# A third column tile in the first product of a sparse-attention and retention block, and a different split of its last steps

## The chip, the cores and the metric

The kernel runs on one core of one Trainium2 chip. The metric is the time of one execution on the device in microseconds (us); lower is better. A time given for a kernel is the median of several runs. Beside it stands the profile of one execution, whose span runs from the first to the last instruction.

## The reference

One layer of a streaming encoder for 512 tokens of width 2048, all in float32. Cut to what matters here:

```python
h = rmsnorm(x, norm_gain)                       # 512 x 2048
aq, ak, av, az, iq, ik, iw, rq, rk, rv, rz, ga, gb = split(h @ w_in)
# iq: 16 heads x 64, ik: 64 (layer-normed), iw: 16
index = sum_over_heads(relu(iq . ik) * iw)      # which 128 keys each query may see
a = sparse_attention(aq, ak, av, top_k(index), rel_bias) * silu(az)
b = retention(rope(rq), rope(rk), rv) * silu(rz)
r = x + (sigmoid(ga) * (a @ w_a_out) + sigmoid(gb) * (b @ w_b_out)) @ w_o
y = r + (p @ w_ple) * sigmoid(r @ w_ple_gate)
out = rmsnorm(y, final_gain)                    # 512 x 2048
```

The change concerns the very first product (the columns for `ik`, `iw` and the first `iq` heads) and the very last step (the final norm of the last tokens and the stores of the output).

## The kernel before

**Number format and layout.** Channels lie on the 128 partitions and the 512 tokens along the free dimension, so x is 16 tiles `xk` of 128 x 512 (256 KB each). Every float32 operand of a product is split into a high part in a reduced format and the rest: `x_split(k)` has ScalarE write `hh` (x times the norm weight `ng`, line 385) and VectorE write `hl` (line 386). Weights are loaded by SyncE's queue into raw tiles (line 115), then split by ScalarE into `wh` (line 136) and by VectorE into `wl` (line 141). One product step is three matmuls: high x high (line 196), high weight x low input (197), low weight x high input (198). The gain of each token, 1/rms, is applied later, so the product can start before the norm is known. `rms_acc` squares each `xk` on ScalarE (line 367) and adds the squares on GpSimd (even k) and VectorE (odd k, line 372).

**Weights come in blocks.** `block(src, chunks, cols)` cuts a weight matrix into units of so many of the 16 k-steps. `split_to(n)` emits the split of all units below n, `load_to(n)` their loads. `wh` and `wl` have three buffers each.

**The step queue.** The order of the work is written by hand. `gemms` (lines 177 to 202) runs over the 16 k-steps, and within each over its column tiles ("jobs"):

```python
for s in order:
    for ps, seq, (_, w, parts, c, _) in zip(pss, seqs, jobs):
        i, k = seq[s]
        if k == 0:
            split_to(i + (ahead or AHEAD) - (late and s > 0))
            load_to(i + AHEAD + LOADS)
        ...                     # three matmuls
        step()
```

After each job of each step, `step()` takes one item from the list `todo` (an item may be `None`) and emits it, so `todo` weaves the other engines' work into the matmul order. `later(n, f)` emits f n steps on. Each engine executes its own instructions in the order in which they are emitted. A list `bg` of background work (the later inputs, the top-k rounds, the bias masks) is drawn from when `todo` has nothing, every few steps.

**The first product.** Loads of `xk` and of the unit weights `w_ik` alternate on SyncE's queue, after the 20 KB of norm weights `g_sb` (line 338). The product has two column tiles: 80 columns (`ps_ikw`: the key of the indexer and its head weights, 512 tokens) and 128 columns (`ps_iq`: two indexer heads, tokens 128 to 511). `w_ik` has 208 columns in units of 2, 2, 4, 4 and 4 k-steps. While the loads arrive, ten warm-up matmuls run on zeros (line 380). Then seven more products give the other 14 indexer heads, tile by tile (`u_iq[1]` to `u_iq[7]`, two units of 8 k-steps each); `iq_split` copies each result out of PSUM with two ScalarE and two VectorE instructions (lines 436 to 439). Behind that, `todo` holds the norm (`f_sum`, `f_rnat`), the keys (`f_keys1` to `3`) and the index scores (`index_tile`).

**The last step.** The first 12 of 16 output channel tiles (`MF`) are ready for all tokens; for tokens 384 to 511 (`C3`) the last 512 channels are computed the other way round, with tokens on partitions (`ps_tg`, `ps_tw`). Their tail is a chain: for two halves of 256 columns a multiply and an add on VectorE (lines 1252, 1253) and a square with a row sum on ScalarE (line 1254); then 1/rms on GpSimd (`rl`, line 1259); its broadcast over PSUM by TensorE (`bb`, line 1263); a store of those 512 channels (`yb`, line 1265); and a multiply of the 12 other tiles by the broadcast, one of four on GpSimd and three on VectorE (lines 1273, 1275), stored by SyncE four tiles at a time (`yo`, line 1276). Earlier, `a_out` has scaled and stored tokens 0 to 383 (lines 1232 to 1238).

Of the kernel before, what the change touches and what calls it, by code (L numbers as in the profile page):

```python
# [13 lines left out]
AF = mybir.ActivationFunctionType  # L14
OP = mybir.AluOpType

L = 512
D = 2048
KT = D // 128
# [15 lines left out]
def block_kernel(tc, xT, pT, posb, posq, w_in, w_v, w_ik, w_a, w_b, w_o, w_ple, w_gate,  # L35
                 w_gt, w_pt, fgb, tab, gains, cst, dec, out, out_a, out_b):
    nc = tc.nc
    pe, dve, act, pool, sp = nc.tensor, nc.vector, nc.scalar, nc.gpsimd, nc.sync

    with contextlib.ExitStack() as ctx:  # L40
# [22 lines left out]
        def tok(t):  # L63
            return slice(128 * t, 128 * t + 128)
# [14 lines left out]
        def block(src, chunks, cols=128):  # L79
            ids, k0 = [], 0  # L80
            for nk in chunks:
                ids.append(len(units))
                units.append((raw(src, k0, nk, cols), None, nk, cols))
                k0 += nk
            return ids
# [67 lines left out]
        todo = collections.deque()  # L153
# [27 lines left out]
        def gemms(jobs, ahead=None, order=None, each=None):  # L181

            pss = [P(j[4]) for j in jobs]
            seqs = [ksteps(j[0]) for j in jobs]
            late = order is not None
            order = order or range(len(seqs[0]))
# [6 lines that stand above are left out]
                    h, l = loaded[i]  # L193
                    a, b = parts[s][0][:, c], parts[s][1][:, c]
                    o = ps[:w.stop - w.start, c]
                    pe.matmul(o, h[:, k, w], a, start=(s == order[0]), stop=False)  # L196
                    pe.matmul(o, h[:, k, w], b, start=False, stop=False)  # L197
                    pe.matmul(o, l[:, k, w], a, start=False, stop=(s == order[-1]))  # L198
                    step()
                if each is not None:  # L200
                    each(s)
            return pss
# [108 lines left out]
        K8 = (8, 8)  # L311
        col = lambda g, m: w_in[g + m]
        AQ, AK, AZ, IQ, RQ, RK, RZ, GA, GB = 0, 8, 16, 24, 32, 40, 48, 56, 72
        u_ik = block(w_ik, (2, 2, 4, 4, 4), 208)
        u_iq = [None] + [block(col(IQ, m), K8) for m in range(1, 8)]
        u_rv, u_av = ([block(w_v[i], (2,) * 8, 512) for i in g] for g in ((0, 1), (2, 3)))
        u_r, u_g = [], []
        for h in range(NH):
# [16 lines left out]


        g_sb = cp.tile([128, 40], F32, name="g_sb")
        sp.dma_start(g_sb, gains)
        ng, fg, gn = g_sb[:, 0:16], g_sb[:, 16:32], g_sb[:, 32:40]
        xs = []  # L340
        for k in range(KT):
            if k in (1, 2, 4, 8, 12):
                load_to(state["raw"] + 1)
            if k < 10:
                t = U("xk")
                sp.dma_start(t, xT[:, k, :])
                xs.append(t)
            elif k % 2 == 0:
                t = B("xk2")
                sp.dma_start(t[:, 0:1024].rearrange("p (a c) -> p a c", a=2), xT[:, k:k + 2, :])  # L350
                xs += [t[:, 0:512], t[:, 512:1024]]
# [68 lines left out]

        for k in range(2, KT):
            todo.append(lambda k=k: x_split(k))
            if k in (4, 5):
                todo.append(None)
            if k == 11:
                todo.extend([None] * 5)
        for k in range(KT):
            todo.extend([lambda k=k: rms_acc(xs[k], k), None])

        ps_ikw, ps_iq0 = gemms([(u_ik, slice(0, 80), hparts, ALL, "ps_ikw"),  # L430
                                (u_ik, slice(80, 208), hparts, slice(128, L), "ps_iq")], 2)

        def iq_split(ps):
            ta = U("ta", F32R)
# [7 lines left out]
        R = {}  # L442
        kraw = U("kraw")
        act.activation(kraw[:80, :], ps_ikw[:80, :], AF.Copy)
        ix = iq_split(ps_iq0)

        def f_sum():
            dve.tensor_add(acc[0], acc[0], acc[1])
# [123 lines left out]
                dve.scalar_tensor_tensor(a, rl[:, :ln], wq[:, t, n:n + 1], a, op0=OP.mult, op1=OP.add)  # L572

        def index_tile(m, ix):
            todo.extend(N3)
            for s in range(2):
                for t in range(1, NT):
                    todo.append(lambda s=s, t=t: index_score(2 * m + s, ix[s], t))

        index_tile(0, ix)  # L580
        for m in range(1, 8):
            ix = iq_split(gemm(u_iq[m], hparts, "ps_iq", slice(128, L)))
            index_tile(m, ix)

# [663 lines left out]
        drain()  # L1248
        sq = U("sq")
        for i in range(2):  # L1250
            c = slice(256 * i, 256 * i + 256)
            dve.tensor_mul(s[:, c], pw[:, c], s[:, c])
            dve.tensor_add(s[:, c], s[:, c], rn[:, c])
            act.activation(sq[:, c], s[:, c], AF.Square, accum_out=r3[:, i:i + 1])
# [9 lines left out]
        act.activation(s, s, AF.Copy, scale=rl)  # L1264
        sp.dma_start(out_b, s)
        b3 = U("b3")
        act.activation(b3[:, 0:128], bb[0][:, 0:128], AF.Copy)
        for q in range(MF // 4):
            o = U("yo")
            for i in range(4):  # L1270
                m = 4 * q + i
                if i == 3:
                    pool.tensor_mul(o[:, tok(i)], ys[m][:, C3], b3[:, 0:128])
                else:
                    dve.tensor_mul(o[:, tok(i)], ys[m][:, C3], bb[1][:, 0:128])
            sp.dma_start(out[:, 4 * q:4 * q + 4, C3], o.rearrange("p (a c) -> p a c", a=4))


MF = 12
# [19 lines left out]
def _layout(x, p, positions, w_in, norm_gain, w_a_out, w_b_out, w_o, ret_gn_gain,  # L1299
            w_ple, w_ple_gate, rel_bias, final_gain):  # L1300
    import numpy as np
    f32 = np.float32

    def tiles(w, c=128):
        k, n = w.shape
        return np.ascontiguousarray(w.reshape(k // 128, 128, n // c, c).transpose(2, 1, 0, 3))

    def chans(v):
        return v.reshape(-1, 128).T

    w = np.asarray(w_in)[0]
    o = {}
    o["xT"] = np.ascontiguousarray(np.asarray(x)[0].T.reshape(KT, 128, L).transpose(1, 0, 2))
    o["pT"] = np.ascontiguousarray(np.asarray(p)[0, 0].T.reshape(2, 128, L).transpose(1, 0, 2))
    pos = np.asarray(positions)[0]
    o["posb"] = np.ascontiguousarray(np.broadcast_to(pos[None, :], (128, L)))
    o["posq"] = np.ascontiguousarray(np.repeat(pos.reshape(128, 4).T, 32, axis=0))
    o["w_in"] = np.concatenate([tiles(w[:, a:b]) for a, b in
                                ((0, 2048), (3072, 5120), (5200, 7248), (8272, 13392))])
    o["w_v"] = np.concatenate([tiles(w[:, a:a + 1024], 512) for a in (7248, 2048)])  # L1320
    o["w_ik"] = np.ascontiguousarray(
        np.concatenate([w[:, 5120:5200], w[:, 4096:4224]], axis=1).reshape(KT, 128, 208).transpose(1, 0, 2))
    o["w_a"] = tiles(np.asarray(w_a_out)[0])
    o["w_b"] = tiles(np.asarray(w_b_out)[0])
    o["w_o"] = tiles(np.asarray(w_o)[0])
    o["w_ple"] = np.ascontiguousarray(
        np.asarray(w_ple)[0].reshape(2, 128, 16, 128).transpose(1, 2, 0, 3).reshape(128, 32, 128))
    o["w_gate"] = tiles(np.asarray(w_ple_gate)[0])
    o["w_gt"] = tiles(np.asarray(w_ple_gate)[0][:, 1536:], 512)
    o["w_pt"] = tiles(np.asarray(w_ple)[0][:, 1536:], 512)  # L1330
    o["fgb"] = np.ascontiguousarray(np.broadcast_to(np.asarray(final_gain)[None, 1536:], (128, 512)))
    tab = np.asarray(rel_bias)
    t = np.zeros((128, 65), f32)
    for q in range(4):
        for b in range(31):
            t[32 * q + b, 8 * q:8 * q + 8] = tab[ROW[b]]
            if b:
                t[32 * q + b, 32 + 8 * q:40 + 8 * q] = tab[ROW[b - 1]]
        t[32 * q:32 * q + 32, 64] = [-1e9] + THR[1:] + [1e9]
    o["tab"] = t  # L1340
    o["gains"] = np.ascontiguousarray(np.concatenate(
        [chans(np.asarray(norm_gain)[0]), chans(np.asarray(final_gain)), chans(np.asarray(ret_gn_gain)[0])], axis=1))
    c = np.zeros((128, 130), f32)
    c[:, :128] = np.eye(128)
    c[:, 128] = np.tile((10000.0 ** (-np.arange(64) / 64.0)).astype(f32), 2)
    c[:, 129] = math.pi / 2
    o["cst"] = c
    s = np.arange(128)[:, None]
    q = np.arange(128)[None, :]
    dec = np.zeros((128, NH, 257))  # L1350
    for h in range(NH):
        g = math.log(1.0 - 2.0 ** (-5.0 - h))
        dec[:, h, :128] = np.where(q // 64 >= s // 64, np.exp(g * np.abs(q - s)), 0.0) * 128.0 ** -0.5
        dec[:, h, 128:256] = np.exp(g * (q + 1.0))
        dec[:, h, 256] = np.exp(g * (127.0 - s[:, 0])) * 128.0 ** -0.5
    o["dec"] = dec.astype(f32)
    return o
# [30 lines left out]
```

## Time and profile before

| | |
|---|---|
| time, median of 3 runs | 1690.11 us (1689.55 to 1690.82) |
| the profiled execution's own time | 1689.83 us |
| its span | 1688.1 us |
| TensorE (PE) busy | 1675.0 us, 99% |
| VectorE (DVE) busy | 1275.3 us, 76% |
| ScalarE (ACT) busy | 863.4 us, 51% |
| GpSimd (POOL) busy | 213.4 us, 13% |
| granted TensorE clock | 0.998 of full |
| moved by DMA | 355.86 MB, 211 GB/s on average |

PEld is TensorE's weight load, which overlaps its matmuls; SPq is the queue of SyncE, which issues most transfers. A timeline row gives the start in us from the span's start, the duration, the engine, the line and operation, the tile written and read, and in brackets how long the engine had been idle and what ended that. Matmuls are pipelined: a 128 x 512 matmul is shown with 0.39 us, but the next one starts 0.23 us after it. So for TensorE the distance between starts counts, not the shown duration.

### The profile page before, as it was taken

What the parts mean: (1) busy time and instruction counts of PE and PEld (TensorE: products, weight loads), DVE (VectorE), ACT (ScalarE), POOL (GpSimd) and SP (SyncE); (2) the same over time, 40 slices, a digit from 0 to 9 for tenths busy, and PEclk for the clock granted to TensorE, in tenths of its full rate; (3) what the DMA queues carried; (4) which work ended last, traced back from release to release, by engine and by line L of the source; (5) the groups of instructions that cost most, each with busy time, mean ns of one, the idle gap of its engine ahead of it and who ended that gap; (6) DMA issues with size and microseconds to landing.
All of it is one profiled execution on the core that took longest, in us unless ns stands there. A gap on an engine that the chain in (4) does not pass through costs nothing.

```text
span 1688.1 us, 25020 instructions
## 1 busy us (share of the span) xinstructions
PE 1675.0 (99%) x9334; PEld 1453.5 (86%) x9334; DVE 1275.3 (76%) x2014; ACT 863.4 (51%) x1278; POOL 213.4 (13%) x216
## 2 busy tenths in 40 slices
PE   9999999999999999999999999999999999999997
PEld 7988888888888888888888888888888888888896
DVE  7787988887887887887887777687768877864453
ACT  7464523555555555555555555566644444463342
POOL 3100000111111111111331111100000111112222
PEclk9999999999999999999999999999999999999999
DMA  7438989788787788787988879998566788733222
GB/s 288 125 105 297 361 323 329 184 223 223 167 224 199 196 215 234 169 211 210 271 219 234 220 197 243 242 360 288 180 204 187 189 229 218 201 118 100 87 63 100
DMA packets 135369, 355.86 MB, mean 211 GB/s; under 512 B 14800, under 2 KB 27088, under 8 KB 135248
## 3 DMA queue, kind: packets, MB, share of 16 engines
q1 hardware_dynamic: 102640, 256.22, 44.0%
q0 software_dynamic: 21376, 77.60, 25.4%
q10 hardware_dynamic: 11232, 20.45, 3.3%
q8 instruction: 73, 1.20, 0.3%
q14 instruction: 48, 0.39, 0.1%
HBM read 301.26 MB, written 52.95 MB: 210 GB/s over the span
## 4 chain that ended last, share of the span: by engine, by line
PE 94%; DVE 3%; ACT 1%; DMA 1%; issue 0%; SPq 0%; POOL 0%; DVEq 0%; ACTq 0%
PE ps_p L258 23%; PE ps_v L258 15%; PE ps_r L258 8%; PE ps_q L258 8%; PE ps_vn L702 3%; PE ps_vn L701 3%; PE ps_vn L703 3%; PE ps_w L196 3%; PE ps_w L197 3%; PE ps_w L198 3%; PE ps_pg L198 3%; PE ps_pg L196 3%; PE ps_pg L197 3%; PE ps_iq L196 1%; PE ps_iq L197 1%; PE ps_iq L198 1%
## 5 line engine op out<-in xcount | busy, mean ns | idle before, releaser
L141 DVE TENSOR_TENSOR wl<-wraw,wh 128x1024 fp32r<-128x1024 f32 (+2 forms) x459 | 560.5, 1229 | 203.5 <-ACT wh L136 197.3
L136 ACT ACTIVATE wh<-wraw 128x1024 fp32r<-128x1024 f32 (+2 forms) x459 | 474.2, 1042 | 272.5 <-DVE wraw L143 132.9
L104 POOL DMA_DIRECT2D wraw<-w_in x120 | 106.3, 961 | 844.2 <-DVE wl L141 437.1
L224 ACT ACTIVATE e<-ps_p 128x512 f32<-128x512 f32 x144 | 86.1, 598 | 164.6 <-PE ps_p L258 162.4
L258 PE MATMUL ps_p<-hs,wh 128*128 128x512 f32 x640 | 161.4, 394 | 0.0
L258 PEld LDWEIGHTS ps_p<-hs,wh 128*128 128x128 f32 x640 | 114.9, 189 | 21.3 <-issue 0.7
L701 PE MATMUL ps_vn<-wh,hh 128*128 128x512 f32 x256 | 99.7, 390 | 0.0
L703 PE MATMUL ps_vn<-wh,hl 128*128 128x512 f32 x256 | 99.7, 389 | 0.0
L702 PE MATMUL ps_vn<-wl,hh 128*128 128x512 f32 x256 | 99.7, 389 | 0.0
L258 PE MATMUL ps_p<-hs,wl 128*128 128x256 f32 x640 | 92.1, 284 | 0.0
L258 PEld LDWEIGHTS ps_p<-hs,wl 128*128 128x128 f32 x640 | 83.1, 192 | 0.5 <-issue 0.4
L258 PE MATMUL ps_r<-hs,wh 128*128 128x512 f32 x320 | 82.3, 395 | 0.2 <-ACT wh L136 0.2
L258 PE MATMUL ps_p<-ha,wh 128*128 128x512 f32 x320 | 80.4, 393 | 0.0
L258 PE MATMUL ps_v<-ha,wh 128*128 128x512 f32 x320 | 80.3, 392 | 0.0
L258 PE MATMUL ps_q<-ha,wh 128*128 128x512 f32 x320 | 80.1, 392 | 0.0
L258 PE MATMUL ps_v<-hs,wh 128*128 128x512 f32 x320 | 79.3, 389 | 0.0
L198 PE MATMUL ps_pg<-rh,wl 128*128 128x512 f32 x192 | 74.8, 390 | 0.0
L197 PE MATMUL ps_pg<-rl,wh 128*128 128x512 f32 x192 | 74.7, 389 | 0.0
L196 PE MATMUL ps_pg<-rh,wh 128*128 128x512 f32 x192 | 74.7, 389 | 0.0
L862 DVE TENSOR_TENSOR go<-e_t 128x256 f32<-128x256 f32 x160 | 68.0, 425 | 5.6
L258 PEld LDWEIGHTS ps_v<-hs,wh 128*128 128x128 f32 x320 | 60.0, 188 | 12.7 <-issue 0.2
L258 PEld LDWEIGHTS ps_v<-ha,wh 128*128 128x128 f32 x320 | 59.4, 188 | 12.3 <-issue 0.3
(350 smaller groups left out, 3500.7 us busy)
## 6 DMA issues: line engine op xcount, KB each, us to landing
wraw<-w_in SPq DMA_DIRECT2D x174, 512.0 KB, 5.5
wraw<-w_in POOLq DMA_DIRECT2D x120, 512.0 KB, 7.8
wraw<-w_v SPq DMA_DIRECT2D x32, 512.0 KB, 5.5
wraw<-w_o SPq DMA_DIRECT2D x32, 512.0 KB, 4.9
wraw<-w_o POOLq DMA_DIRECT2D x24, 512.0 KB, 6.8
wraw<-w_gate SPq DMA_DIRECT2D x24, 512.0 KB, 4.1
hd<-hs SPq DMA_DIRECT2D x32, 256.0 KB, 5.1
hs<-hd SPq DMA_DIRECT2D x32, 256.0 KB, 5.5
```

Source lines behind the costliest of these rows:

```text
L104: pool.dma_start(out=raw_tiles[r], in_=src[:, k0:k0 + 8, :], accum_op=OP.add)
L136: act.activation(h, raw, AF.Copy)
L141: dve.tensor_sub(l, raw, h.bitcast(F32))
L196: pe.matmul(o, h[:, k, w], a, start=(s == order[0]), stop=False)
L197: pe.matmul(o, h[:, k, w], b, start=False, stop=False)
L198: pe.matmul(o, l[:, k, w], a, start=False, stop=(s == order[-1]))
L224: act.activation(E[n], src, AF.Copy)
L258: pe.matmul(o[:, c], w[:, k], X[PRODUCTS[n]][k][:, c], start=(n < 4 and part == 0 and k == 0), stop=(part == parts[1] and k == 7), skip_gr ...
L701: pe.matmul(pss[t], a[:, tok(t)], h[:, k], start=(s == 0), stop=False)
L702: pe.matmul(pss[t], a[:, tok(t)], l[:, k], start=False, stop=False)
L703: pe.matmul(pss[t], b[:, tok(t)], h[:, k], start=False, stop=(s == KT - 1))
L862: dve.tensor_add(o[:, q], c0, c1)
```

## The change

Three edits.

First, the block `w_ik` gets 128 more columns (336 in place of 208), so the first product has a third column tile; the separate product for `u_iq[1]` goes. Its units become 1, 2, 2, 2, 3, 3 and 3 k-steps, with the loads placed accordingly among those of x. The squares of k = 0 to 5 are placed between the splits of x instead of behind the last of them, and the splits of x come one for every three column tiles.

Second, the norm weights are loaded by ScalarE's queue, and no longer ahead of the first x tile on SyncE's.

Third, the halves of 256 columns in the last norm become 384 and 128; of each four output tiles the first, no longer the last, goes to GpSimd; VectorE reads the broadcast that is made first; the second of three stores is issued by ScalarE, and the third is cut in two, one from each queue.

```diff
-        u_ik = block(w_ik, (2, 2, 4, 4, 4), 208)
-        u_iq = [None] + [block(col(IQ, m), K8) for m in range(1, 8)]
+        u_ik = block(w_ik, (1, 2, 2, 2, 3, 3, 3), 336)
+        u_iq = [None, None] + [block(col(IQ, m), K8) for m in range(2, 8)]
...
-        sp.dma_start(g_sb, gains)
+        act.dma_start(g_sb, gains)
...
-            if k in (1, 2, 4, 8, 12):
+            if k in (1, 2, 3, 5, 7, 9, 12):
                 load_to(state["raw"] + 1)
...
         for k in range(2, KT):
             todo.append(lambda k=k: x_split(k))
-            if k in (4, 5):
-                todo.append(None)
-            if k == 11:
-                todo.extend([None] * 5)
-        for k in range(KT):
+            if k > 2:
+                todo.extend([None, None if k % 2 else lambda k=k: rms_acc(xs[k // 2 - 2], k // 2 - 2)])
+        for k in range(6, KT):
             todo.extend([lambda k=k: rms_acc(xs[k], k), None])
-        ps_ikw, ps_iq0 = gemms([(u_ik, slice(0, 80), hparts, ALL, "ps_ikw"),
-                                (u_ik, slice(80, 208), hparts, slice(128, L), "ps_iq")], 2)
+        ps_ikw, *ps_iq01 = gemms([(u_ik, slice(0, 80), hparts, ALL, "ps_ikw")]
+                                 + [(u_ik, slice(a, a + 128), hparts, slice(128, L), "ps_iq") for a in (80, 208)], 2)
...
-        ix = iq_split(ps_iq0)
+        ix = [iq_split(ps) for ps in ps_iq01]
...
-        index_tile(0, ix)
-        for m in range(1, 8):
+        for m in range(2):
+            index_tile(m, ix[m])
+        for m in range(2, 8):
             ix = iq_split(gemm(u_iq[m], hparts, "ps_iq", slice(128, L)))
             index_tile(m, ix)
...
-            c = slice(256 * i, 256 * i + 256)
+            c = (slice(0, 384), slice(384, 512))[i]
...
-        act.activation(b3[:, 0:128], bb[0][:, 0:128], AF.Copy)
+        act.activation(b3[:, 0:128], bb[1][:, 0:128], AF.Copy)
         for q in range(MF // 4):
             o = U("yo")
             for i in range(4):
                 m = 4 * q + i
-                if i == 3:
+                if i == 0:
                     pool.tensor_mul(o[:, tok(i)], ys[m][:, C3], b3[:, 0:128])
                 else:
-                    dve.tensor_mul(o[:, tok(i)], ys[m][:, C3], bb[1][:, 0:128])
-            sp.dma_start(out[:, 4 * q:4 * q + 4, C3], o.rearrange("p (a c) -> p a c", a=4))
+                    dve.tensor_mul(o[:, tok(i)], ys[m][:, C3], bb[0][:, 0:128])
+            o = o.rearrange("p (a c) -> p a c", a=4)
+            if q < MF // 4 - 1:
+                (sp, act)[q % 2].dma_start(out[:, 4 * q:4 * q + 4, C3], o)
+            else:
+                for e, a in ((act, 0), (sp, 2)):
+                    e.dma_start(out[:, 4 * q + a:4 * q + a + 2, C3], o[:, a:a + 2])
```

In `index_tile` the three empty steps ahead of a tile's scores are left out for tiles 0 and 1, and the host lays the 128 further columns of `w_in` into `w_ik`.

More of the change, by code (lines that the diff above doesn't have):

```diff
@@ L574, in index_tile @@
         def index_tile(m, ix):
-            todo.extend(N3)
+            if m > 1:
+                todo.extend(N3)
             for s in range(2):
@@ L1321, in _layout @@
     o["w_ik"] = np.ascontiguousarray(
-        np.concatenate([w[:, 5120:5200], w[:, 4096:4224]], axis=1).reshape(KT, 128, 208).transpose(1, 0, 2))
+        np.concatenate([w[:, 5120:5200], w[:, 4096:4352]], axis=1).reshape(KT, 128, 336).transpose(1, 0, 2))
     o["w_a"] = tiles(np.asarray(w_a_out)[0])
```

## The prediction

> **What bounds the kernel now.** I read the page first, then the busy times by stretches of 25 us, then the timelines of the first 36 and the last 15 us, where the change lies.
>
> ```profile
> span 1688.1 us, 25020 instructions
> ...
> PE 94%; DVE 3%; ACT 1%; DMA 1%; issue 0%; SPq 0%; POOL 0%; DVEq 0%; ACTq 0%
> ```
> ```profile
> 0.00:25.00 25.00, 22.35 (x94) 15.07 (x95) 16.65 (x26) 18.92 (x29) 0.97 (x5) 1.00 0.93 336
> ...
> sum 1675.00, PE 1671.95 PEld 1451.38 DVE 1268.48 ACT 860.85 POOL 208.84; mean PE 24.95 PEld 21.66 DVE 18.93 ACT 12.85 POOL 3.12
> ```
>
> TensorE carries 94% of the chain that ended last. Of the first 1675.00 us it is idle for 3.05, and 2.65 of those lie in the first 25 us. So the kernel is a stream of matmuls with a ragged start and a tail behind its last matmul. The change takes no matmul away: what it can win is the raggedness of the start and a part of the tail, a few us of 1690. I take 0.2% (3.4 us) as what a measurement can tell from no change.
>
> **The first product: what is lost there.**
>
> ```profile
> 0.75 0.40 SPq L338 DMA_DIRECT2D g_sb<-gains  x1
> ...
> 1.20 0.42 SPq L346 DMA_DIRECT2D xk<-xT  x1
> ...
> 1.36 4.45 PE L380 MATMUL ps_warm<-warm 128*128 128x512 bf16 x10 [1.36 <-DVE warm L375]
> ...
> 2.61 0.43 SPq L115 DMA_DIRECT2D wraw<-w_ik  x1
> ...
> 3.08 0.91 SPq L346 DMA_DIRECT2D xk<-xT  x2
> ...
> 3.96 0.72 ACT L385 ACTIVATE hh<-xk,g_sb 128x512 fp32r<-128x512 f32 x1 [1.71 <-DMA xk<-xT]
> ...
> 5.36 0.74 PE L196 MATMUL ps_ikw<-hh,wh 128*80 128x512 f32 x1
> ...
> 5.93 0.40 PE L197 MATMUL ps_ikw<-hl,wh 128*80 128x512 f32 x1
> ...
> 6.75 0.72 ACT L385 ACTIVATE hh<-xk,g_sb 128x512 fp32r<-128x512 f32 x1 [1.45 <-DMA xk<-xT]
> ...
> 15.29 0.39 PE L196 MATMUL ps_ikw<-hh,wh 128*80 128x512 f32 x1
> ...
> 27.47 0.34 PE L196 MATMUL ps_iq<-hh,wh 128*128 128x384 f32 x1
> ...
> 35.80 0.33 PE L196 MATMUL ps_iq<-hh,wh 128*128 128x384 f32 x1
> ```
>
> From 15.29 to 27.47 us ten steps of two column tiles run undisturbed: 12.18 / 10 = 1.218 us a step. The second product (27.47 to 35.80 us, 16 steps of one tile) takes 0.521 us a step. The first matmul is shown from 5.36 us with 0.74 us, but the second starts at 5.93, one spacing of 0.23 us after 5.70: until then the warm-up matmuls still stream (ten of them from 1.36 us on), so 5.70 is the real start. Sixteen undisturbed steps would end at 5.70 + 16 x 1.218 = 25.19 us; they end at 27.47. So 2.28 us are lost to hungry steps, and this is all that the third tile can win. The groups of instructions in the first 36 us say for what TensorE waits:
>
> ```profile
> L196 PE MATMUL ps_ikw<-hh,wh 128*80 128x512 f32 x16 | 6.8, 423 | 0.6 <-ACT hh L385 0.4 <-ACT wh L136 0.2
> L197 PE MATMUL ps_ikw<-hl,wh 128*80 128x512 f32 x16 | 6.4, 403 | 0.3 <-DVE hl L386 0.3
> L198 PE MATMUL ps_ikw<-hh,wl 128*80 128x512 f32 x16 | 6.3, 396 | 0.4 <-DVE wl L141 0.4
> ```
>
> It waits for the splits of x and of weights, which wait for transfers: supply is late by a fixed amount early on, and a step with more matmuls gives it time to catch up.
>
> **The first product after.** A step has 1.218 + 0.521 = 1.739 us of matmuls; 16 make 27.82 us, and without a stall the three tiles end at 33.52 us, where now they end at 35.80. Next the stalls that stay.
>
> The start doesn't move. Without the norm weights ahead of it the first x tile is issued 0.45 us sooner (0.75 in place of 1.20), so its split could start at 3.5 us, but the warm-up matmuls hold TensorE to 5.70 anyway. The load on ScalarE's queue costs nothing: bounded by SyncE's 0.40 us an issue, it puts ScalarE's first work back by less than half a us, and ScalarE was idle for 1.71 us before 3.96.
>
> The second step is due at 5.70 + 1.74 = 7.44 us. It needs the second x tile and the second weight unit, now 672 columns wide (two k-steps of 336). The landings, of the weights issued at 2.61 and of the two x tiles issued from 3.08 us on (the second at 3.08 + 0.91 / 2 = 3.5):
>
> ```profile
> wraw<-w_ik SPq DMA_DIRECT2D x1, 208.0 KB, 4.7
> ```
> ```profile
> xk<-xT SPq DMA_DIRECT2D x2, 256.0 KB, 5.0
> ```
> ```profile
> L385 ACT ACTIVATE hh<-xk,g_sb 128x512 fp32r<-128x512 f32 x16 | 10.8, 716 | 5.0 <-DMA xk<-xT 4.9
> L367 ACT ACTIVATE sq<-xk 128x512 f32<-128x512 f32 x14 | 7.7, 616 | 0.0
> ...
> L136 ACT ACTIVATE wh<-wraw 128x832 fp32r<-128x832 f32 x3 | 2.7, 884 | 0.0
> ...
> L136 ACT ACTIVATE wh<-wraw 128x416 fp32r<-128x416 f32 x2 | 1.1, 541 | 0.1
> ```
> ```profile
> L386 DVE SCALAR_TENSOR_TENSOR hl<-xk,g_sb,hh 128x512 fp32r<-128x512 f32 x16 | 11.2, 749 | 6.1 <-ACT hh L385 6.1
> ...
> L141 DVE TENSOR_TENSOR wl<-wraw,wh 128x832 fp32r<-128x832 f32 x3 | 3.1, 1023 | 0.0
> L141 DVE TENSOR_TENSOR wl<-wraw,wh 128x416 fp32r<-128x416 f32 x2 | 1.2, 586 | 0.0
> ```
>
> Now the second weight unit is the fourth transfer of the product: 928 KB in all, landed at 2.61 + 4.7 = 7.3 us; the fourth x tile ends the first 1440 KB at 3.5 + 5.0 = 8.5 us. That is 0.0024 us a KB. After the change the second unit ends the first 1016 KB (256 + 168 + 256 + 336), 88 KB more, but issued 0.45 us sooner: 7.3 + 0.2 - 0.45 = 7.05 us. Between the widths of 416 and 832 the splits cost 0.82 ns a column on ScalarE and 1.05 on VectorE, so 672 columns take 0.75 and 0.86 us. ScalarE's part ends at 7.8 us: a stall of 0.36 us. The low weights end at 8.66; TensorE wants them after two spacings, at 8.26: a stall of 0.4. Together 0.8 us with the restarts.
>
> From there supply outruns demand. A pair of steps (3.48 us of matmuls) needs on ScalarE two splits of x (10.8 / 16 = 0.68 us each), 0.75 for 672 weight columns and a square (7.7 / 14 = 0.55), 2.7 us; on VectorE 2 x 11.2 / 16 + 0.86 + 0.7 for an addition = 3.0; and of transfers 2 x (256 + 168) = 848 KB, 2.0 us. The thinnest place is the third weight unit. ScalarE splits it behind the fourth x tile, which now ends 1864 KB: 8.5 + 424 x 0.0024 - 0.45 = 9.1 us, split by 9.8; the unit's high part is done at 10.55, its low part at 11.4. TensorE wants that at 7.44 + 0.8 + 2 x 1.739 + 0.46 = 12.2. Cover 0.8 us.
>
> So the three tiles end at about 33.52 + 0.8 = 34.3 us in place of 35.80: **1.5 us gained**. Bounds: 2.3 with no stall at all; 0.4 if the second unit lands a us later than I put it (the second x tile, only the third transfer now, is seen at 6.75 us, hardly sooner than the fourth).
>
> **The seam behind it, at nothing.** At the end of the product ScalarE must empty three PSUM tiles, not two, before it splits the next weights.
>
> ```profile
> 27.14 0.59 ACT L444 ACTIVATE kraw<-ps_ikw 80x512 f32<-80x512 f32 x1 [1.42 <-PE ps_ikw L198]
> ...
> 28.17 0.49 ACT L437 ACTIVATE tz<-ps_iq 64x384 fp32r<-64x384 f32 x1
> ```
> ```profile
> 29.84 2.36 DVE L141 TENSOR_TENSOR wl<-wraw,wh 128x1024 fp32r<-128x1024 f32 x2
> ```
>
> Now the first low weights behind the seam are ready 3.6 us after it (29.84 + half of 2.36 against 27.47). Two more ScalarE copies of 0.49 us, less 0.52 because the 80-column tile is finished one tile sooner, make it 4.1. They are wanted after eight steps and two spacings, 8 x 0.521 + 0.35 = 4.5 us. Cover 0.4 us; if it is gone, the excess shows once.
>
> **The middle, at nothing.** The product loses 16 one-tile steps elsewhere and gains them here, so the count of steps up to the values stays, and so do weight units (5 + 14 = 7 + 12). In the order of instructions the position and rotation work falls two weight units later, into the values' stage, and background items shift by up to three units until the retention heads end. TensorE idles 0.4 us there now (3.05 less 2.65); I allow as much either way.
>
> **The tail, 0.2 us.**
>
> ```profile
> 1677.52 0.42 DVE L1252 TENSOR_TENSOR sg<-ps_tw,sg 128x256 f32<-128x256 f32 x1
> ```
> ```profile
> 1680.99 0.71 PE L1263 MATMUL ps_b<-cs,rl 128*128 128x128 f32 x4 [3.68 <-POOL rl L1259]
> ```
> ```profile
> 1681.74 1.87 DVE L1275 TENSOR_TENSOR yo<-y,ps_b 128x128 f32<-128x128 f32 x9 [1.21 <-PE ps_b L1263]
> ```
> ```profile
> 1682.49 1.62 SPq L1276 DMA_DIRECT2D y<-yo  x3
> ```
> ```profile
> 1682.00:1683.00 1.00, 0.00 (x0) 0.00 (x0) 1.00 (x7) 0.00 (x0) 1.00 (x3) 0.50 1.03 370
> 1683.00:1684.00 1.00, 0.00 (x0) 0.00 (x0) 0.61 (x4) 0.00 (x0) 0.22 (x1) 0.50 0.99 323
> ...
> 1685.00:1686.00 1.00, 0.00 (x0) 0.00 (x0) 0.00 (x0) 0.00 (x0) 0.00 (x0) 0.50 1.06 298
> 1686.00:1687.00 1.00, 0.00 (x0) 0.00 (x0) 0.00 (x0) 0.00 (x0) 0.00 (x0) 0.50 0.49 139
> ```
>
> In a stretch's row the last two numbers are the share of the 16 DMA engines and GB/s. With 384 and 128 columns the first multiply and add grow by what the second pair shrinks (128 columns are 0.21 us by the multiplies of `yo`, 1.87 / 9, against 0.42 for 256), and only the last square, no longer than half of the other, is shorter: 0 to 0.2 us. Reading the first broadcast starts VectorE's nine multiplies up to half of 0.71 us sooner. So the last store could be issued some 0.4 us earlier. But the DMA engines are full until 1686.5: earlier issues only wait. What remains is the dip at 1683, 323 GB/s between 370 and the 298 of the small rows: about 0.2 us. Bounds: 0.6 gained (if the small rows went at 370 GB/s, 3 x 256 KB, 786,000 bytes, would take 2.1 us, not 2.6, and the dip went too), or 0.3 lost to mixing the two queues. The Trainium skill speaks against this edit: "DMA: Bandwidth & Descriptors", section "Issuing engines are not separate DMA queues", says that transfers issued by different engines run on the same 16 DMA engines and that several issuers only save issue time; by it the two queues bring 0 here, and the shares of 0.99 to 1.06 agree with it.
>
> **Sum.** The profiled execution took 1689.83 us (span 1688.1 and 1.7 around it), 0.28 below the median of the runs, 1690.11. 1689.83 - 1.5 - 0.2 = 1688.1; for a median 1688.4, which I forecast.
>
> **Rivals.**
> (a) Supply stays as late: the wider units land later by what the longer steps give, the stall of the second step is 2 us and the whole start is worth 0.3. Speaks for it: the second x tile's late landing at 6.75. Against: rates rise quickly after it. Time 1690.11 - 0.3 - 0.2 = 1689.6.
> (b) Two queues do widen the tail (0.6) and the start has no stall (2.3), with 0.4 from the middle: 1686.8. Against: the full DMA shares. Past 3.4 us it would need a gain that no row shows.
> (c) Slower: GpSimd's additions of squares now fall among the splits of x, no longer behind them, and slow VectorE.
>
> ```profile
> 35.53 2.31 DVE L141 TENSOR_TENSOR wl<-wraw,wh 128x1024 fp32r<-128x1024 f32 x1
> ```
>
> Beside such additions this split took 2.31 us, not half of 2.36: 1.1 more. Up to four fall into the product while splits are due (k = 2, 4, 6, 8). If VectorE had no slack, 4.4 us would go to TensorE: 1690.1 - 1.7 + 4.4 = 1692.8. It decides once VectorE's work (some 20 us by the durations above, in 28) passes the supply's pace; before k = 8 only one such addition falls, with over 1 us in hand. To pass +3.4 us it would have to strike the seam as well.
> (d) The change doesn't do what it says: TensorE's order does show the third tile in each step, so only the tail's part can be empty; that lies in the forecast.
>
> **Chances.** Forecast 0.62; (a) 0.15; (b) 0.13, of which 0.07 past 3.4 us; (c) 0.10, of which 0.06 past it. So faster by over 0.2% 0.07, within 0.87, slower 0.06. The range takes in (b) at its lower end and (a) with the runs' scatter of 0.7 at its upper: 1686.7 to 1690.4, which leaves out 0.17 or so.
>
> **What would show it.** Right: the third product's first matmul (now at 35.80) near 34.3, one pair of stalls at the second step, no idle at 38 to 39 us, and DMA shares at 1.0 to about 1.5 us before the end. Wrong: idle TensorE between 12 and 34 us waiting for `wl`; idle behind the seam; rates above 330 GB/s in the last 2 us of transfers.

## The result, and the profile after

| | before | after |
|---|---|---|
| time, median of 7 runs each | 1690.18 us (1689.55 to 1690.82) | 1695.41 us (1694.34 to 1696.77) |
| ratio to before | | 1.0031, 95% interval 1.0021 to 1.0040 |
| span of the profiled execution | 1688.1 us | 1693.6 us |
| first matmul of the product that follows `iq` tiles 0 and 1 | 35.80 us | 34.83 us |
| last matmul of `ps_tw` | 1676.93 us | 1682.55 us |

The change made the kernel 5.2 us slower, outside the range of 1686.7 to 1690.4. Its start, which the prediction worked out, did gain, and the tail took as long as before; the loss lies in the middle, which the prediction had set to nothing. The page's first line and its chain, and the waits of TensorE, longest first (what waited, on whom, us in total, times, longest):

```profile
span 1693.6 us, 25022 instructions
...
PE 94%; DVE 2%; ACT 2%; DMA 1%; issue 1%; SPq 0%; POOL 0%; ACTq 0%; DVEq 0%
```
```profile
PE ps_r L258 <- ACT wh L136: 3.9, 1, 3.9
...
PE ps_ikw L196 <- ACT wh L136: 0.8, 1, 0.8
PE ps_p L258 <- DVE wl L141: 0.7, 1, 0.7
```

Before, the chain gave ScalarE 1%; it has 2% now. The first of these waits was 0.2 us before, and the last is not among the waits of before.

**Where the time went.** ScalarE's gate stores (line 872: the sigmoids of `ga` and `gb`, written out to memory) come at the same place of the work in both kernels, so their start times are a clock of the progress. Together with TensorE's first matmul of later stages:

| mark | before | after | difference |
|---|---|---|---|
| end of the first products | 35.80 | 34.83 | -0.97 |
| first `ps_rs` matmul of the retention (line 750) | 308.55 | 307.39 | -1.16 |
| second gate store | 326.58 | 326.46 | -0.12 |
| 14th gate store | 513.98 | 513.86 | -0.12 |
| 17th gate store | 572.02 | 577.48 | +5.46 |
| first `ps_pt` matmul (line 967) | 1130.35 | 1135.97 | +5.62 |
| last `ps_tw` matmul | 1676.93 | 1682.55 | +5.62 |
| end of the span | 1688.06 | 1693.64 | +5.58 |

So the start won 1 us, two places lost 1.04 us (308 to 327 us) and 5.58 us (514 to 577 us), and the tail is the same within 0.04. The larger loss in the timeline after:

```profile
529.31 0.33 ACTq L872 DMA_DIRECT2D sgb<-go  x1
...
530.16 1.76 POOL L104 DMA_DIRECT2D wraw<-w_in  x2 [1.30 <-DVE wl L141]
530.31 3.90 SPq L639 DMA_DIRECT2D scr<-bev  x4
...
534.76 0.63 ACT L871 ACTIVATE go<-go 128x512 f32<-128x512 f32 x1 [1.33 <-DVE go L862]
535.25 4.48 SPq L639 DMA_DIRECT2D scr<-bev  x4
...
542.16 0.33 ACTq L872 DMA_DIRECT2D sgb<-go  x1
...
542.53 0.60 ACT L224 ACTIVATE pv<-ps_v 128x512 f32<-128x512 f32 x1 [7.14 <-DMA scr<-bev]
543.03 1.05 ACT L136 ACTIVATE wh<-wraw 128x1024 fp32r<-128x1024 f32 x1
...
544.13 2.08 PE L258 MATMUL ps_r<-hs,wh 128*128 128x512 f32 x4 [3.93 <-ACT wh L136]
```

Read from the bottom: TensorE stood 3.93 us for a high part of weights; ScalarE made it late because it had itself stood 7.14 us, and what ended that was the landing of a store of bias rows (`scr<-bev`, rows of the attention's bias, stored by SyncE, line 639). Between its last work (the sigmoid of a gate, done at 535.4) and 542.5 ScalarE has one instruction, its own store of that gate (542.16). The chain of the same stretch names the piece:

```profile
531.03 1.00 SPq L639
...
532.08 10.01 DMA scr<-bev
...
542.11 0.02 ACTq L872
...
542.16 0.33 ACTq L872
```

The third bias store needed 10.01 us to land (to 542.09), then a wait of ScalarE ended (542.11), and its store went out. A completion semaphore is a counter that a transfer raises when it has landed, and for which an engine can wait. In this program, and so in its trace, each transfer of SyncE and of ScalarE names one of eight such semaphores, in turn over both engines, and waits until the transfer eight places earlier has landed; GpSimd's transfers name eight others. Numbered from 0 to 7, the gate store has 5, and so has the third bias store, eight transfers ahead of it:

```
SyncE   scr<-bev    3        SyncE   scr<-bev    1
SyncE   scr<-bev    4        SyncE   scr<-bev    2
SyncE   scr<-bev    5  <--   SyncE   scr<-bev    3
SyncE   scr<-bev    6        SyncE   wraw<-w_in  4
SyncE   wraw<-w_in  7        ScalarE sgb<-go     5  <-- waits
SyncE   scr<-bev    0
```

The same stretch of the kernel before, and the issue-to-landing rows of these eight stores (64 KB each) before and after:

```profile
523.00 1.26 SPq L639 DMA_DIRECT2D scr<-bev  x2
525.58 4.10 SPq L639 DMA_DIRECT2D scr<-bev  x6
...
535.57 0.33 ACTq L872 DMA_DIRECT2D sgb<-go  x1
...
535.94 0.60 ACT L224 ACTIVATE pv<-ps_v 128x512 f32<-128x512 f32 x1 [0.40 <-ACT go L871]
```
```profile
scr<-bev SPq DMA_DIRECT2D x8, 64.0 KB, 2.1
```
```profile
scr<-bev SPq DMA_DIRECT2D x8, 64.0 KB, 8.6
```

Before, the burst went out 7 us earlier, ahead of the weight loads, and landed in 2.1 us; the gate store at 535.57 found its semaphore free, and ScalarE went on 0.40 us after the sigmoid. ScalarE's own queue did not hold it there, though its store of 531.29 was still on its way (in the trace it landed at 541.14). After, the burst falls among weight loads of two queues and lands in 8.6 us.

TensorE lost more than it stood. Rows of 1 us each (the number before the last two is the granted clock):

```profile
544.00:545.00 1.00, 0.87 (x2) 0.78 (x3) 0.89 (x1) 1.00 (x3) 0.00 (x0) 0.50 0.73 225
545.00:546.00 1.00, 1.00 (x3) 0.71 (x3) 0.79 (x2) 0.51 (x1) 0.00 (x0) 0.50 0.99 374
546.00:547.00 1.00, 1.00 (x4) 0.80 (x3) 0.97 (x2) 0.00 (x0) 0.00 (x0) 0.50 1.18 326
547.00:548.00 1.00, 1.00 (x8) 0.89 (x7) 1.00 (x2) 0.00 (x0) 0.00 (x0) 0.91 0.87 165
548.00:549.00 1.00, 1.00 (x10) 1.00 (x10) 0.97 (x4) 0.89 (x1) 0.00 (x0) 1.00 0.83 267
```

The clock was half from 543.8 to 547.2 us, and TensorE worked for 3.1 us of that: 0.87 x 0.5 + 0.5 + 0.5 + 0.09 = 1.5 us of work lost. 3.93 + 1.5 = 5.4 of the 5.58 us.

**Why it moved.** All bias stores come from the background list `bg`, which is served when `todo` is empty. Counting steps as the program emits them: the squares of x end 7 steps later (step 60, not 53), the index tiles have 6 empty entries fewer, so `todo` runs out 1 step later. From then on `bg` is exactly one item behind: 2 steps later where one item comes every 2 steps, 3 where every 3, and 18 steps (about 7 us) where every 18. That is the whole shift.

The smaller loss has the same root. VectorE after, then TensorE, then VectorE before:

```profile
308.77 0.69 DVE L600 MAX8 m<-isc 128x8 f32<-128x512 f32 x1
...
310.28 0.43 DVE L603 TENSOR_SCALAR mneg<-isc 128x512 bf16<-128x512 f32 x1
310.62 1.22 DVE L141 TENSOR_TENSOR wl<-wraw,wh 128x1024 fp32r<-128x1024 f32 x1
```
```profile
311.89 1.22 PE L258 MATMUL ps_p<-hs,wl 128*128 128x256 f32 x8 [0.72 <-DVE wl L141]
```
```profile
309.92 0.28 DVE L616 TENSOR_SCALAR mk<-relf,thr 128x128 bf16<-128x128 f32 x1
310.12 1.22 DVE L141 TENSOR_TENSOR wl<-wraw,wh 128x1024 fp32r<-128x1024 f32 x1
```

Where a bias mask of 0.28 us stood ahead of a low weight part, the last top-k round stands now (308.77 to 310.6, 1.85 us), and TensorE waits 0.72 us. By the distance of starts it is 0.88 of the 1.04 us: `ps_p` follows `ps_r`'s low part after 1.83 us (310.06 to 311.89), before after 0.95 (311.24 to 312.19).

### The profile page after: what moved, and what is told of

It is laid out like the page before. It is cut to its first block, busy times and chain, and to the rows that moved or that the text cites. A ratio compares the mean times of both kernels' runs of the same rounds, so it can differ in the third digit from the quotient of the medians.

```text
span 1693.6 us, 25022 instructions
## 1 busy us (share of the span) xinstructions
PE 1676.5 (99%) x9334; PEld 1454.6 (86%) x9334; DVE 1275.3 (75%) x2014; ACT 861.8 (51%) x1278; POOL 213.7 (13%) x216
## 4 chain that ended last, share of the span: by engine, by line
PE 94%; DVE 2%; ACT 2%; DMA 1%; issue 1%; SPq 0%; POOL 0%; ACTq 0%; DVEq 0%
PE ps_p L258 24%; PE ps_v L258 15%; PE ps_r L258 8%; PE ps_q L258 8%; PE ps_vn L703 3%; PE ps_vn L701 3%; PE ps_vn L702 3%; PE ps_w L197 3%; PE ps_w L196 3%; PE ps_w L198 3%; PE ps_pg L198 3%; PE ps_pg L197 3%; PE ps_pg L196 3%; PE ps_iq L196 1%; PE ps_iq L198 1%; PE ps_iq L197 1%
## 5 line engine op out<-in xcount | busy, mean ns | idle before, releaser
L258 PEld LDWEIGHTS ps_r<-hs,wh 128*128 128x128 f32 x320 | 58.0, 192 | 14.1 <-ACT wh L136 4.1
```

The source lines that it names most:

```text
L258: pe.matmul(o[:, c], w[:, k], X[PRODUCTS[n]][k][:, c], start=(n < 4 and part == 0 and k == 0), stop=(part == parts[1] and k == 7), skip_gr ...
```

## The experiments

Theory A: the background list, one item late, costs the time; the burst of bias stores holds ScalarE's gate store through the shared semaphore. Theory B: the wide first product itself, by its load on VectorE or the order of transfers, costs it. Theory C: the tail's two queues or the norm weights' queue do.

| kernel | median us | ratio to before, 95% interval |
|---|---|---|
| noop | 1695.55 | 1.0034 (1.0022 to 1.0047) |
| onestep | 1689.36 | 0.9995 (0.9986 to 1.0004) |
| gate_sp | 1710.52 | 1.0117 (1.0102 to 1.0133) |
| bias18 | 1695.27 | 1.0030 (1.0018 to 1.0041) |
| gate_late | 1689.74 | 1.0000 (0.9991 to 1.0008) |
| stores18 | 1689.89 | 0.9999 (0.9990 to 1.0007) |
| noop3 | 1692.63 | 1.0016 (1.0007 to 1.0025) |
| tailonly | 1689.68 | 0.9998 (0.9989 to 1.0007) |
| gains | 1689.31 | 0.9994 (0.9985 to 1.0002) |
| wide | 1690.10 | 1.0001 (0.9992 to 1.0010) |
| gate_pool | 1689.23 | 0.9995 (0.9986 to 1.0004) |
| wide_again | 1690.30 | one run, before 1690.44 |

**noop: the late list alone, in the kernel before.**
```diff
+        bg.append(lambda: None)
         bg.append(lambda: xn_load(0))
```


> The kernel before, with one empty item put at the head of the background list; nothing else. Every later background item then comes one place later, at the same steps as in the changed kernel (2 steps later at rate 2, 3 at rate 3, 18 at rate 18, 9 at rate 9). Theory A (the place of the background list costs the time: a burst of bias stores gets ahead of ScalarE's gate store, which waits some 7 us, and TensorE stands 3.9 us and then runs at a low clock): the kernel loses the 6.6 us that the changed kernel lost in its middle, so 1696 to 1697.5, with a wait of TensorE of 3 to 4.5 us near 545 us and the first attention instruction of the position work some 5 to 7 us later. Theory B (the wide first product itself, or its load on VectorE and the DMA order that it leaves behind, costs the time): 1690.2, within 0.5. Theory C (the tail's two queues or the norm weights' queue cost it): 1690.2 as well.

Measured 1695.55, 0.5 below what was expected, and within 0.2 of the changed kernel. One empty item, and none of the three edits, brings the loss: by the marks above 1.06 us at the first place and 4.92 at the second, 6.0 of the changed kernel's 6.6. Its waits of ScalarE and of TensorE, and its clock behind them:
```profile
ACT pv L224 <- DMA scr<-bev: 6.3, 1, 6.3
```
```profile
PE ps_r L258 <- ACT wh L136: 3.1, 1, 3.1
```
```profile
545.00:546.00 1.00, 1.00 (x4) 0.81 (x3) 0.79 (x2) 0.41 (x1) 0.00 (x0) 0.50 0.98 373
```

**onestep: the changed kernel with the list back in its place.**
```diff
-... + [f_keys3] + N3 * 2)
+... + [f_keys3] + N3 + [None] * 2)
```


> The changed kernel, with one empty entry fewer behind the last step of the index keys, so that the background list starts one step sooner; from the seventh item on every background item then comes at the very step at which it comes in the kernel before. Theory A: the stall near 545 us is gone, what remains is the gain at the start (1.0 us) and at the tail (0.1 us): 1688.5 to 1689.5, ratio to before 0.9990 to 0.9997. Theory B or C: 1694 to 1696.5, as the changed kernel.

Measured 1689.36, 6.0 below the changed kernel. The waits at 311 and 545 us are gone from its list of waits, and the eight bias stores land in 2.1 us as before. B and C fall, and theory A holds for all but some 0.6 us of the loss: from the 14th to the 17th gate store this trace still takes 58.61 us, before 58.04, with no new wait. `gains` and `wide_again`, whose list stands where it stood, take 58.39 and 58.37, so the list need not be the cause; it was not traced. This version has all three edits and beats the changed kernel, as `gate_late` and `gate_pool` do below; against the kernel before its interval takes in 1.

**bias18: only the bias banks one item later, in the kernel before.**
```diff
-            bg.append(lambda two=two: later(6, lambda: bias_banks(two)))
+            bg.append(lambda two=two: later(24, lambda: bias_banks(two)))
```


> The kernel before with the background list where it was; only the last step of each pair of bias banks (its matmuls, copies and stores) is put off by 24 steps in place of 6, so 18 steps, one item at the rate of that stage; the masks on VectorE stay. Theory A: the burst of bias stores falls where it falls in the changed kernel: 1694 to 1697.5 with the wait of TensorE near 545 us. If VectorE's masks or the norm work in the list cost the time: 1690.2, within 0.7. Theory B or C: 1690.2.

Measured 1695.27. The masks and the norm work kept their places, and there is no wait at 311 us. In a median execution the bias banks bring nearly all of the loss. The trace is of the fastest of the six executions (1693.43 us): TensorE stood 3.5 us near 543 us, and its clock stayed full behind that.
```profile
ACT pv L224 <- DMA scr<-bev: 6.7, 1, 6.7
```
```profile
PE ps_r L258 <- ACT wh L136: 3.7, 2, 3.5
```

**gate_sp: the gate stores from SyncE.**
```diff
-                act.dma_start(dst[i], o)
+                sp.dma_start(dst[i], o)
```


> The changed kernel with the list where it is (one item late), but the stores of the sigmoid gates issued by SP and not by ScalarE. Theory A in its detailed form (ScalarE stands in order behind its own store, which waits for a bias store that is still landing): ScalarE no longer stands, the weight split comes in time, the wait of 3.9 us near 545 us goes; SP stands instead, ahead of weight loads that are three units ahead: 1688.5 to 1691. Theory A' (the late list costs by something else, for instance by VectorE's masks or the bias matmuls in front of the product): 1694 to 1696.5. Theory B or C: 1694 to 1696.5.

Measured 1710.52, a miss. The wait at 545 us did go (TensorE is busy for all of 520 to 560 us), but SyncE now stands in order ahead of its weight loads, 40 times, for the sigmoids, and ScalarE stands 35.7 us in sum for weights:
```profile
SPq L872 <- ACT go L871: 243.8, 40, 15.8
```
It moves the standing to a worse engine and decides nothing.

**gate_late: one store, 30 steps later, in the changed kernel.**
```diff
-        def to(dst, func):
+        def to(dst, func, lag=0):
             ...
-                act.dma_start(dst[i], o)
+                later(lag * i, lambda: act.dma_start(dst[i], o))
...
-                gate_pair(u_g[n], to(d[m:m + 2], AF.Sigmoid))
+                gate_pair(u_g[n], to(d[m:m + 2], AF.Sigmoid, 30 * (n == 7)))
```


> The changed kernel with the list where it is (one item late); one transfer alone is moved: the last store of the first eight sigmoid gates, which ScalarE issues, comes 30 steps (some 10 us) later, when the first burst of bias stores should have landed. Theory A in its detailed form (ScalarE stands in order behind this one store): ScalarE's 7.1 us of waiting and TensorE's 3.9 us near 545 us are gone, and with them the low clock behind: 1688.5 to 1690.5. If the burst of bias stores costs in another way (the bandwidth it takes, SP's queue, the weights late behind it): 1693 to 1696.5.

Measured 1689.74. Bias burst, list and queues are those of the changed kernel, the eight stores still take 8.0 us to land; one transfer of ScalarE at another place takes away 5.7 us. At its new place (543.14) it still makes ScalarE stand 1.2 us for a bias store, but TensorE does not stand for that.

**gate_pool: the same store at its old place, but from GpSimd.**
```diff
-                act.dma_start(dst[i], o)
+                (pool if last and i else act).dma_start(dst[i], o)
...
+                gate_pair(u_g[n], to(d[m:m + 2], AF.Sigmoid, n == 7))
```


> The changed kernel with the list where it is (one item late); the last store of the first eight sigmoid gates is issued at its old place, but by GpSimd, whose transfers do not share completion semaphores with those of SP and ScalarE. If the shared semaphore held ScalarE: the store is issued within 1.5 us of its data (534 to 537 us), while the bias stores are still landing, ScalarE and TensorE don't stand, 1688.8 to 1690.5. If the store waits for the transfers of the bias burst in another way (full DMA engines, the buffer, the memory behind it): GpSimd stands as ScalarE did, and the weights that it loads behind it come late: 1692 to 1697.

Measured 1689.23. The store goes out 0.4 us after its data (sigmoid from 534.29 for 0.63 us) and lands in 6.7 us while the bias stores beside it still take 8.3, so neither the DMA engines nor the memory held it. By itself this leaves ScalarE's own queue beside the semaphore; that it was the semaphore, the wait of the changed kernel's trace shows (542.11, behind the landing at 542.09):
```profile
535.28 0.58 POOL L872 DMA_DIRECT2D sgb<-go  x1 [3.82 <-ACT go L871]
```
```profile
sgb<-go POOLq DMA_DIRECT2D x1, 256.0 KB, 6.7
```

**stores18: only SyncE's bias stores 18 steps later, in the kernel before.**
```diff
-                later(8 + 4 * n, lambda dst=dst, n=n: sp.dma_start(...))
+                later(26 + 4 * n, lambda dst=dst, n=n: sp.dma_start(...))
```


> The kernel before, with masks, bias matmuls and copies where they were; only SP's stores of the bias banks are put off by 18 steps. Theory A: the first eight of them fall between the same two gate stores as in the changed kernel, and ScalarE stands behind the second: 1693.5 to 1697, with a wait of TensorE of 3 to 4.5 us near 540 us. If the bias matmuls or the copies in their later place are what costs: 1690.2, within 0.7.

Measured 1689.89, a miss, and instructive. SyncE runs ahead of the emission and had stood waiting for the bias copies, so 18 steps of order moved the stores by only 3.6 us:
```profile
526.57 2.54 SPq L639 DMA_DIRECT2D scr<-bev  x4
...
529.78 3.07 SPq L639 DMA_DIRECT2D scr<-bev  x4
```
The transfer eight places ahead of the gate store (535.50) was here the fourth of them; in the trace it was issued at 528.51 and had landed at 531.04. The place in the order alone does not hold ScalarE: that transfer must also land later than the store is ready to go.

**noop3: the list two items late.**
```diff
+        bg.extend([lambda: None] * 3)
         bg.append(lambda: xn_load(0))
```


> The kernel before with three empty items at the head of the background list: in the stretch with rate 18 every item then comes 36 steps later than before, two items late and not one. Theory A: the first burst of bias stores starts near 537 us, behind the gate store of 535.6 us and with no other store of ScalarE until 572 us, so nothing stands behind it: 1690.2, within 0.8, although the list is later than in the changed kernel. If lateness of the list as such costs (more at the end of the list, masks or norm work in a dearer place): 1696 or more.

Measured 1692.63: between the two. Over the burst nothing is lost: the marks stand at +0.82 against before at the 14th gate store (514.80) and at the 17th (572.84), as theory A has it for a burst behind both gate stores. But the late list costs elsewhere: 1.55 us at the top-k rounds (from the `ps_rs` mark to the second gate store)
```profile
311.84 1.21 PE L258 MATMUL ps_p<-hs,wl 128*128 128x256 f32 x8 [0.29 <-DVE wl L141]
319.22 0.95 PE L258 MATMUL ps_p<-hs,wl 128*128 128x256 f32 x6 [0.75 <-DVE wl L141]
```
and 0.84 us between the gate stores of 662 and 705 us, in gaps of at most 0.4 us whose cause I did not trace. The trace is of the fastest execution (1691.54 us); the 1.1 us from there to the median are in no trace. So late is not dear as such, and not free either.

**tailonly, gains, wide: the three edits.** `tailonly` is the kernel before with the new tail and the norm weights on ScalarE's queue, `gains` with the norm weights alone, `wide` the third column tile alone with the list in its place.

> The kernel before with the change's tail (the last tokens in 384 and 128 columns, stores from two queues) and with the norm weights loaded by ScalarE's queue; the first product is as before. Theory A: 1690.0, within 0.5: the tail gained 0.1 us in the changed kernel's trace, and the list is where it was. Theory C (tail or norm weights cost the time): 1694 to 1696.5.

> The kernel before, with the norm weights loaded by ScalarE's queue and nothing else changed. The prediction's start (the third tile wins the hungry steps, the norm weights' queue moves nothing, since the warm-up matmuls hold TensorE): the second product's first matmul stays at 27.47 us. The other reading (each transfer of SP comes 0.45 us sooner, so the second x tile is in time for the second step): it comes at 26.4 to 26.6, the stall of the second step is gone, and the gate stores of the middle come 0.9 to 1.1 us sooner: 1689.0 to 1689.9.

> The third column tile alone: the changed kernel with the norm weights on SP's queue and the tail as before, and with one empty entry fewer so that the background list stands where it stood. The prediction's start: its 1.5 us are the third tile's, so the next product's first matmul (35.80 before) at 34.3 to 34.9. The other reading (the 1.0 us come from the norm weights' queue): 35.3 to 35.9, and 1689.7 to 1690.3.

> The third column tile alone once more, for a profile: the first one was of the slowest of its eleven executions (1692.56 us against a median of 1690.10). If the third tile alone gains nothing, an ordinary execution has the next product's first matmul (35.80 before) at 35.3 to 36.3 and TensorE standing 0.8 to 1.5 us at the second step; if it gains what the prediction gave it, at 34.3 to 34.9.

None of the three differs measurably from before, so theory C is out on its own too, and what each brings can be read only in the traces. The second product's first matmul, 27.47 before, in `gains` (first row) and in `tailonly` (second); and the next product's first matmul (35.80 before) in `wide_again`, whose second weight unit made TensorE stand:
```profile
26.78 0.34 PE L196 MATMUL ps_iq<-hh,wh 128*128 128x384 f32 x1
```
```profile
26.45 0.34 PE L196 MATMUL ps_iq<-hh,wh 128*128 128x384 f32 x1
```
```profile
8.79 0.46 PE L196 MATMUL ps_ikw<-hh,wh 128*80 128x512 f32 x1 [0.55 <-ACT wh L136]
...
35.44 0.35 PE L196 MATMUL ps_iq<-hh,wh 128*128 128x384 f32 x1
```
Against the one trace of before, the norm weights' queue is worth 0.7 to 1.0 us and the third tile 0.36. Single executions scatter: the mark of 35.80 lies at 35.60 to 35.80 in the five traces with the old start (`before`, `noop`, `bias18`, `stores18`, `noop3`) and at 34.18 to 34.83 in the five with the whole new one (`after`, `onestep`, `gate_sp`, `gate_late`, `gate_pool`), so the start is worth 0.8 to 1.6 us, by the middle values 1.2. The profile of `wide` itself is of the slowest of its eleven executions: TensorE stood 1.75 us for the second weight unit, its clock then fell to half for 3.4 us, and the mark came at 37.41. So the third tile alone can also lose.
```profile
9.27 0.46 PE L196 MATMUL ps_ikw<-hh,wh 128*80 128x512 f32 x1 [1.75 <-ACT wh L136]
```
`gains` came out at 26.78, a little above the 26.4 to 26.6 expected; the sense holds.

## Why the prediction was wrong

**The middle, at nothing: this step failed.** It saw that background items shift, and priced that by TensorE's idle time of before: "TensorE idles 0.4 us there now (3.05 less 2.65); I allow as much either way." That idle time bounds what a shift can win. It bounds no loss: a stage with no idle time can get a new wait of any length. The shift cost 6.6 us (1.04 + 5.58). The step allowed for a shift of up to three weight units, and did not ask what a shifted item lands on; the shift was one item, which at one item per 18 steps is 7 us, and the two gate stores of 531.29 and 535.57 were within that reach of the burst. What the trace of before did show, and the step didn't look at, are the rows of lines 639 and 872 above: eight transfers of SyncE, the last issued 5.9 us ahead of a store of ScalarE, the engine on which the weights wait.

**The first product: right in sign and nearly in size, but put down to the wrong edit.** The forecast was 1.5 us; the trace has 0.97, `onestep` 1.30 (34.50), and the traces together 0.8 to 1.6. The rows of the first two steps after:

```profile
1.36 3.85 PE L380 MATMUL ps_warm<-warm 128*128 128x512 bf16 x10 [1.36 <-DVE warm L375]
...
5.03 0.46 PE L196 MATMUL ps_ikw<-hh,wh 128*80 128x512 f32 x1
...
5.87 0.72 ACT L385 ACTIVATE hh<-xk,g_sb 128x512 fp32r<-128x512 f32 x1 [0.90 <-DMA xk<-xT]
...
7.36 0.76 ACT L136 ACTIVATE wh<-wraw 128x672 fp32r<-128x672 f32 x1 [0.76 <-DMA wraw<-w_ik]
...
8.17 0.46 PE L196 MATMUL ps_ikw<-hh,wh 128*80 128x512 f32 x1 [0.81 <-ACT wh L136]
```

Here the second weight unit landed at 7.36, not 7.05, and the stall for it was 0.81, not 0.36, with 0.20 for the low part where 0.4 was forecast; in `onestep` the unit's split starts at 7.03 and the stall is 0.46, so executions scatter about as much as the forecast was off. "The start doesn't move" is what failed. The warm-up matmuls do hold the first matmul (5.36 before, 5.25 in `gains`, 5.03 here, where the ten took 3.85 us and not 4.45). But the second x tile's split starts at 5.87 where it was 6.75 (5.60 in `gains`, 6.65 in `wide_again`, which has the norm weights on SyncE's queue): that is where the norm weights' queue pays, and by these traces it pays more than the third tile. The stall for the wider second unit (0.55 in `wide_again`) takes back a part of the tile's gain. The Trainium skill, "DMA: Bandwidth & Descriptors", section "Issuing engines are not separate DMA queues", says that several issuing engines save only the time of issuing, usually small; here that time is 0.45 us of SyncE, and the start gained 0.7 to 1.0 in `gains` and `tailonly`.

**The seam: right.** No wait stands at 38 to 39 us, nor anywhere from 10 to 34 us, so rival (c), GpSimd's additions, had the sign and not the cause. Rival (a)'s 0.3 us for the start lies below all five traces.

**The tail: no gain.** From the last matmul of `ps_tw` to the end of the span it took 11.13 us before (1688.06 - 1676.93) and 11.09 after: 0.04 where 0.2 was forecast. Over all traces it took 11.10 to 11.32 us with the old tail and 11.06 to 11.28 with the new one, so the edit brought nothing that shows. VectorE's last multiplies did start 0.3 us sooner (4.51 us behind that matmul, 4.81 before), but DMA stays full to 1.5 us before the end, at 283 to 306 GB/s: the earlier stores only waited, and the second queue widened nothing:

```profile
1689.00:1690.00 1.00, 0.00 (x0) 0.00 (x0) 0.00 (x0) 0.00 (x0) 0.00 (x0) 0.50 1.00 306
1690.00:1691.00 1.00, 0.00 (x0) 0.00 (x0) 0.00 (x0) 0.00 (x0) 0.00 (x0) 0.50 1.02 283
1691.00:1692.00 1.00, 0.00 (x0) 0.00 (x0) 0.00 (x0) 0.00 (x0) 0.00 (x0) 0.50 1.05 289
```

With the list in its place the forecast of 1688.4 would have met 1689.36, inside its range, though only 0.87 of the 1.7 us that it promised (1690.23 to 1689.36, within the noise). What carried the time out of the range is the list.

## What to carry to other kernels

When a change alters how many steps a woven work list takes, count at which step each later item comes out, in both versions, before costing anything else: one item late can be 18 steps. For each burst that moves, list the in-order transfers and engines within reach of the shift, above all stores of an engine that also feeds the bottleneck, and price a new wait by how long that burst takes to land, not by the idle time of today. If such a shift is a side effect, take it out with one empty entry and measure the edit alone.

## What the runs showed of the hardware

A store of ScalarE stood 7.1 us for a transfer that SyncE had issued, because in this program both use the same eight completion semaphores in turn; issued from GpSimd, whose transfers use others, it went out 0.4 us after its data. The same eight stores of 64 KB landed in 2.1 us (median) where the DMA engines were 0.20 to 0.51 busy (523 to 530 us, before), and in 8.6 us among weight loads (0.94 to 1.00 busy, 530 to 543 us, after). And 3.9 us of idle time cost TensorE 1.5 us more at half clock. The Trainium skill, "TensorE: Matmul & The Clock Gate", section "Part 1: The HAM clock gate", puts the fall to half after about 3.4 us without work and the return after about 3.4 us of work. The half clock lasted 3.4 us in the changed kernel, in `noop` and in `wide`, which agrees (in the changed kernel TensorE worked for 3.1 of them). The fall did not go by the length of one idle stretch: it came after 3.12 us in `noop`, 0.7 us after TensorE had gone back to work, and in `wide` after stretches of 1.75 and 0.20 us; after 3.49 us in `bias18` it did not come.
